# Layer 0 experts: context products gathered into fewer, longer groups on TensorE

## Chip, cores and metric

The kernel runs on one core of a Trainium2 chip. The metric is device microseconds (us) of one execution; lower is better. A profiled execution gives the rows that are quoted below. The engines are PE (TensorE, matrix products; its weight loads are listed as PEld), ACT (ScalarE), DVE (VectorE), POOL (GpSimd) and SP, whose queue issues most DMA loads.

## What is computed

A two-layer backbone over 1024 latent tokens and 256 context tokens of width 1024. Layer 0 mixes tokens with two recurrent head groups, layer 1 with attention, and each layer ends in a mixture of 16 experts. An expert picks its tokens itself (128 latent tokens and, in layer 0 alone, 32 context tokens), and adds its result to their rows:

```python
def expert_choice_ffn(h, w_router, w_gate, w_up, w_down):
    B, T, _ = h.shape
    cap = CAP_FACTOR * T // N_EXPERTS
    aff = jax.nn.softmax((h @ w_router).astype(jnp.float32), axis=-1)
    g, idx = lax.top_k(jnp.swapaxes(aff, 1, 2), cap)
    ...
    hid = jax.nn.silu(jnp.einsum('becd,edf->becf', xg, w_gate)) * jnp.einsum('becd,edf->becf', xg, w_up)
    y = jnp.einsum('becf,efd->becd', hid, w_down) * g[..., None].astype(h.dtype)
    return jnp.zeros_like(h).at[bidx, idx].add(y)
```

All arrays are float32. The three weights of an expert are 1024x1024 each, 12 MB together.

## The kernel before

**Chunks.** `experts` walks the 16 experts of a layer. An expert's weights come in twelve chunks of 1 MB, [128, 2048] in SBUF: for each half of the 1024 hidden columns a gate and an up chunk for the first 512 rows (q = 0) and for the last 512 (q = 1), eight in all, and then four down chunks. `weight_chunk` issues the load of a chunk on SP's queue into a raw buffer (`wc`), has ACT round it to fp32r (`wch`) and DVE subtract that from the raw chunk (`wcl`). The pair wch and wcl is called a split pair here. Raw buffers and split pairs are rings: a load waits until the last reader of the buffer's previous chunk is done, a split until the last product with the pair's previous chunk is done. Before, layer 0 has five raw buffers (`nraw`) and four split pairs (`nsplit`).

**Latent products.** The 128 latent tokens' products are made as three fp32r products per 128 weight rows (`mm3`, L138 to L140: high by high, high by low, low by high), each 128x128 by 128x512, into `acc`. A chunk takes 12 of them. They read the split pair alone. The text calls them A.

**Context products.** The 32 context tokens fill only 32 of the array's 128 columns. `mm_context` (L1143) multiplies them in fp32 straight with the raw chunk, and puts the products of even and odd k and of the two matrices m into four column strips (rows 0, 32, 64, 96 of `cg`), so that four run beside each other. Each fp32 product shows as two instructions in the trace. These read the raw buffers, and so hold them. The text calls a run of such products that stands between other work on PE a group, C.

**Order.** PE also transposes: the gathered tokens (`xg`, `xgc`), the hidden activations (`sil` of latent tokens, `hc` of context tokens), and it makes the next expert's row numbers from one-hot products (`rt_hot`, L1075). Every engine works through a fixed list in order; a scheduler makes the lists when the program is built, so that products may end up a little apart from where the code calls them. After the sixteenth expert PE makes part of layer 1's modulation (`mod`, L296, 32 columns wide too), and layer 1 begins with the rows that the last expert has added to (`ye`, then the scatter into `xl`). Layer 1's experts have no context products and run with three split pairs and thirteen raw buffers.

The ring of five raw buffers lies in a pool (`ring`) that exists before the experts' own pool; further raw buffers (`spare_chunk`, as many as `spare` says for the layer) lie in the experts' pool.

Of the kernel before, what the change touches and what calls it, by code (L numbers as in the profile page):

```python
# [23 lines left out]
KT = 8  # L24
# [85 lines left out]
class Kernel:  # L110
# [5 lines left out]
    every = 4  # L116
    xbufs, on_act, on_pool, zfirst, xfirst, nat = 10, (1, 5), (0, 2, 4, 6), 9, 0, 7
    pooled, gated = (2, 0), (0, 2)
    spare = (0, 5)
    ahead = 7  # L120
    by_act, by_pool = (1, 3, 5), (0, 2, 4)
    turned, eased = (0, 1), (2,)
# [1029 lines left out]
    def experts(self, l, routes, hs, xs, m5s, ring, pool, psum):  # L1152

        nc, io = self.nc, self.io
        two = len(routes) == 2
# [52 lines left out]
        def gate_up_chunk(e, half, q, w):  # L1208
            src = w[e, 512 * q:512 * q + 512, 512 * half:512 * half + 512].rearrange("(k p) f -> p k f", p=128)
            return self.weight_chunk(l, ring, pool, src, [128, 4, 512])  # L1210

        def wide_chunk(e, q, w):

            src = w[e, 256 * q:256 * q + 256, :].rearrange("(p a) f -> p a f", a=2)
            return self.weight_chunk(l, ring, pool, src, [128, 2, D])
# [12 lines left out]
        def gate_up(e, half, q, x, acc, cg):  # L1228
            xt, xct = x
            c = []  # L1230
            for m, w in enumerate((wg, wu)):
                c.append(early.pop(0) if early else gate_up_chunk(e, half, q, w))
                for kk in range(4):
                    k = 4 * q + kk
                    self.mm3(acc[:, m], (xt[0][:, k, :], xt[1][:, k, :]), (c[m][1][:, kk, :], c[m][2][:, kk, :]),
                             k == 0, k == KT - 1)
            if two:
                for kk in range(4):
                    k = 4 * q + kk
                    self.mm_context(cg, xct, [c[m][0][:, kk, :] for m in range(2)], k)  # L1240

        def both(acc):

# [31 lines left out]
        def down(e, q, ht, hct, acc, cy):  # L1275
            if two:
                src = wd[e, 256 * q:256 * q + 256, :].rearrange("(k p) f -> p k f", p=128)
                raw, hi, lo = self.weight_chunk(l, ring, pool, src, [128, 2, D])
            else:
                _, hi, lo = wide_chunk(e, q, wd)  # L1280
            for kk in range(2):
                k = 2 * q + kk
                for m in range(2):
                    o = slice(512 * m, 512 * m + 512)
                    self.mm3(acc[:, m], (ht[0][:, k, :], ht[1][:, k, :]), (hi[:, kk, o], lo[:, kk, o]),
                             k == 0, k == KT - 1)
            if two:
                for kk in range(2):
                    k = 2 * q + kk
                    self.mm_context(cy, hct, [raw[:, kk, 512 * m:512 * m + 512] for m in range(2)], k)  # L1290

        def add_rows(i, idx, gate, y, acc):
            nc.vector.scalar_tensor_tensor(y, acc, gate, m5s[i], op0=OP.mult, op1=OP.mult)  # L1293
            nc.gpsimd.indirect_dma_start(out=rows[i], out_offset=bass.IndirectOffsetOnAxis(ap=idx, axis=0),  # L1294
                                         in_=y, in_offset=None, compute_op=OP.add)

        picked = {}
        self.chunks = 0
        self.extra = [self.spare_chunk(l, pool) for _ in range(self.spare[l])]
        if not two:  # L1300
# [35 lines left out]
        for e in range(NE):  # L1336
            hct = pool.tile([128, KT, 32], F32, name="hct", bufs=2) if two else None
            accs = lambda: (psum.tile([128, 2, 512], F32, name="acc", tag="acc", bufs=2),
                            psum.tile([128, 512], F32, name="cg", tag="cg", bufs=2) if two else None)
            a0 = accs()  # L1340
            gate_up(e, 0, 0, x, *a0)
            if e + 1 < NE:
                nxt = pick(e + 1)
            gate_up(e, 0, 1, x, *a0)
            h0 = activate(*a0)
            a1 = accs()
            gate_up(e, 1, 0, x, *a1)
            ht = [pool.tile([128, KT, 128], F32R, name=f"ht{j}", bufs=1) for j in range(2)]
            turn(0, h0, ht, hct)
            gate_up(e, 1, 1, x, *a1)  # L1350
            h1 = activate(*a1)
            if e + 1 < NE:
                x = prep(*nxt)
            ay = accs()
            down(e, 0, ht, hct, *ay)
            turn(1, h1, ht, hct)
            for q in range(1, 4):
                down(e, q, ht, hct, *ay)
# [551 lines left out]
    def build(self, stop=None):  # L1910
        tc, io = self.tc, self.io
        pools = lambda stack, name, **kw: stack.enter_context(
            tc.tile_pool(name=name, bufs=1, reuse_waits="tile", **kw))
        pe = {mybir.EngineType.PE}
        with ExitStack() as ctx:
            self.ctx = ctx
            self.nraw, self.nsplit = 5, 4
            self.constants()
            self.xd = [self.scratch("xl", [TL, D]), self.scratch("xc", [TC, D])]
            self.hd = [self.scratch("hl", [TL, D]), self.scratch("hc", [TC, D])]  # L1920
            self.od = self.scratch("od", [8, 128, TL])
            self.qrd = self.scratch("qrd", [8, 8, 128, 64])
            raws = ExitStack()
            with ExitStack() as right:
                with ExitStack() as left:
                    pa = pools(left, "l0a")
                    ps = pools(left, "l0ps", space=PSUM)

                    class Twice:
                        def tile(self, shape, dt, name, tag, bufs=2):  # L1930
                            return ps.tile(shape, dt, name=name, tag=tag, bufs=2)
                    psum = Twice()
                    self.layer0(pa, psum)
                    if stop == "l0mix":
                        return
                    self.route_constants(pools(ctx, "rc", side="right"))
                    mc = pools(right, "m0c", side="right")
                    ring = pools(right, "m0r", side="right")
                    pool = pools(left, "m0m")
                    left.enter_context(tc.manual_schedule(engines=pe))  # L1940

                    def bank(kind):
                        tag = {"acc": "sA", "tp": "tp", "rl": "mm"}[kind]
                        return psum.tile([128, 2, 512] if tag == "sA" else [128, 512], F32, kind, tag)

                    rest = self.mod_round(1, 5, pool, psum, "mm", lambda: self.ring_chunk(ring), width=1024,
                                          tag="rx", bufs=2)
                    routes = self.tail(0, self.fetch_recurrent, self.wo, pool, bank, mc, pools(left, "m0t", side="right"), rest)
                if stop == "l0":
                    return  # L1950
                self.raws, self.wd_raw = pools(raws, "l1w"), []
                self.moe(0, routes, ring)
            self.layer1(raws)
            if stop == "mla":
                return
            with ExitStack() as right:
                mc = pools(right, "m1c", side="right")
                self.nraw, self.nsplit = self.nraw1, 3
                ring = pools(right, "m1r", side="right")
                with ExitStack() as left:  # L1960
                    pool = pools(left, "m1m")
                    psum = pools(left, "m1p", space=PSUM)
                    left.enter_context(tc.manual_schedule(engines=pe))
                    wo = [pool.tile([128, KT, D], F32R, name=f"wo{j}") for j in range(2)]
                    bank = lambda kind: psum.tile([128, 2, 512] if kind == "acc" else [128, 512], F32, name=kind,
                                                  bufs=2)
                    tags = ("rx", "rxm", "rx", "rxm", "rh", "m2", "m4", "m3")
                    stage = lambda k: pool.tile([128, D], F32, name="owr", tag=tags[k], bufs=1 if k > 3 else 2)
                    routes = self.tail(1, self.fetch_attention, wo, pool, bank, mc, pools(left, "m1t", side="right"),
                                       weights=self.out_weights(*wo, stage, io["w_o"][0]))  # L1970
                self.moe(1, routes, ring)
# [123 lines left out]
```

## Time and profile before

| what | us |
|---|---|
| median of 3 runs (lowest to highest) | 3352.9 (3351.01 to 3357.59) |
| the profiled execution's own time | 3350.71 |
| its span from first to last instruction | 3348.9 |
| first product of layer 0's experts to the last C | 1091.7 to 1923.9 |

The profiled execution is 2.2 us below the median, and its span lacks 1.8 us of its time. In the rows a time after an engine's name is a start in us from the span's beginning, then the duration; matmuls overlap, so what one costs is read from start to next start.

### The profile page before, as it was taken

To read this page: it belongs to the slowest core of one execution; us is meant where nothing else is said; L and a number is where in the kernel's file an instruction comes from. 1 tells how busy PE (TensorE), PEld (TensorE's weight loads), DVE (VectorE), ACT (ScalarE), POOL (GpSimd) and SP (SyncE) were. 2 spreads that over 40 slices of the span, in tenths; PEclk is the share of its full clock that TensorE was granted. 3 is DMA by queue.
4 is the path that set the end of the run, shared out by engine and by line. 5 is a ranking of instruction groups with operands and counts; after the bars stand their busy time and mean duration, and the time that the engine had idled before them with its cause. 6 is when DMAs were issued, how large, how long until landed. Compare 5 with 4: busy or idle time off the path is not lost.

```text
span 3348.9 us, 50379 instructions
## 1 busy us (share of the span) xinstructions
PE 3084.0 (92%) x19910; PEld 2370.4 (71%) x19910; DVE 2263.6 (68%) x3526; ACT 1681.5 (50%) x2405; POOL 653.8 (20%) x730
## 2 busy tenths in 40 slices
PE   5999989898896999999999979999998969999997
PEld 4878767786674566666666668888887758887775
DVE  4774463535657676776776666766666588988887
ACT  4444433544322465565555543555554247766675
POOL 3134452426212111111111010000000110111111
PEclk8999999999898999999999989999999979999999
DMA  6112144134753677878788732010005569999995
GB/s 209 47 32 61 42 151 151 43 100 170 259 175 127 223 263 266 267 275 266 270 272 265 270 97 53 23 29 22 19 15 187 192 244 373 374 363 355 372 358 185
DMA packets 252798, 624.92 MB, mean 187 GB/s; under 512 B 47876, under 2 KB 107482, under 8 KB 222866
## 3 DMA queue, kind: packets, MB, share of 16 engines
q1 hardware_dynamic: 227154, 545.17, 45.4%
q0 software_dynamic: 25408, 76.54, 8.1%
q8 instruction: 156, 2.56, 0.3%
q14 instruction: 80, 0.66, 0.1%
HBM read 560.71 MB, written 60.92 MB: 186 GB/s over the span
## 4 chain that ended last, share of the span: by engine, by line
PE 56%; DVE 4%; ACT 3%; DMA 2%; issue 2%; POOL 0%; SPq 0%; POOLq 0%; ACTq 0%; DVEq 0%
PE acc L138 12%; PE acc L140 11%; PE acc L139 11%; PE cg L1143 6%; PE tp L138 2%; PE tp L139 2%; PE tp L140 2%; PE tp L1784 2%; PE tp L1195 1%; PE tp L1265 1%; PE s L1753 1%; DVE wcl L145 1%; PE s L138 1%; PE s L140 1%; PE s L139 1%
## 5 line engine op out<-in xcount | busy, mean ns | idle before, releaser
L145 DVE TENSOR_TENSOR wcl<-wc,wch 128x2048 fp32r<-128x2048 f32 x380 | 874.1, 2308 | 258.6 <-ACT wch L144 257.3
L144 ACT ACTIVATE wch<-wc 128x2048 fp32r<-128x2048 f32 x380 | 727.9, 1919 | 430.1 <-PE acc L140 160.7
L139 PE MATMUL acc<-wcl,xt 128*128 128x512 f32 x1024 | 408.1, 399 | 1.9 <-DVE wcl L145 1.9
L138 PE MATMUL acc<-wch,xt 128*128 128x512 f32 x1024 | 405.1, 404 | 1.1 <-ACT xt L144 1.1
L140 PE MATMUL acc<-wch,xt 128*128 128x512 f32 x1024 | 405.8, 397 | 0.0
L138 PEld LDWEIGHTS acc<-wch,xt 128*128 128x128 f32 x1024 | 194.0, 189 | 72.3 <-issue 17.6
L139 PEld LDWEIGHTS acc<-wcl,xt 128*128 128x128 f32 x1024 | 193.7, 189 | 46.4 <-DVE wcl L145 4.0
L140 PEld LDWEIGHTS acc<-wch,xt 128*128 128x128 f32 x1024 | 193.4, 189 | 45.2
L139 PE MATMUL acc<-wcl,ht 128*128 128x512 f32 x512 | 204.8, 400 | 8.1 <-DVE wcl L145 8.1
L138 PE MATMUL acc<-wch,ht 128*128 128x512 f32 x512 | 211.5, 413 | 0.4 <-ACT wch L144 0.4
L140 PE MATMUL acc<-wch,ht 128*128 128x512 f32 x512 | 205.7, 402 | 0.0
L138 PE MATMUL mm<-ahi,w 128*128 128x512 f32 (+1 forms) x480 | 182.9, 381 | 0.0
L140 PE MATMUL mm<-ahi,w 128*128 128x512 f32 (+1 forms) x480 | 173.5, 362 | 0.0
L139 PE MATMUL mm<-alo,w 128*128 128x512 f32 (+1 forms) x480 | 173.5, 361 | 0.0
L1161 POOL DMA_INDIRECT xg<-hl,rt_i x32 | 83.1, 2596 | 422.9 <-issue 173.0
L1294 POOL DMA_INDIRECT xl<-ye,rt_i x31 | 69.7, 2249 | 468.5 <-DVE ye L1293 468.5
L138 PE MATMUL mm<-w,ahi 128*128 128x256 f32 (+1 forms) x480 | 148.5, 309 | 2.6 <-DVE tm L432 2.6
L144 ACT ACTIVATE pt<-tp 128x512 fp32r<-128x512 f32 (+1 forms) x192 | 98.5, 529 | 101.7 <-PE tp L1784 100.5
L145 DVE TENSOR_TENSOR pt<-tp,pt 128x512 fp32r<-128x512 f32 (+1 forms) x192 | 113.7, 594 | 44.8 <-ACT pt L144 44.7
L1143 PE MATMUL cg<-wc,xct 128*32 128x512 f32 x1024 | 138.7, 599 | 0.0
L140 PE MATMUL mm<-w,alo 128*128 128x256 f32 (+1 forms) x480 | 137.9, 287 | 0.0
L139 PE MATMUL mm<-w,ahi 128*128 128x256 f32 (+1 forms) x480 | 137.7, 287 | 0.0
(530 smaller groups left out, 7084.7 us busy)
## 6 DMA issues: line engine op xcount, KB each, us to landing
wc<-in_w_gate SPq DMA_DIRECT2D x128, 1024.0 KB, 7.5
wc<-in_w_up SPq DMA_DIRECT2D x128, 1024.0 KB, 6.0
wc<-in_w_down SPq DMA_DIRECT2D x128, 1024.0 KB, 5.7
w<-in_w_mod SPq DMA_DIRECT2D x32, 1024.0 KB, 5.0
craw<-in_w_in SPq DMA_DIRECT2D x40, 256.0 KB, 3.1
wm<-in_w_mod SPq DMA_DIRECT2D x8, 1024.0 KB, 10.6
wc<-in_w_mod SPq DMA_DIRECT2D x8, 1024.0 KB, 10.2
xl<-rxm POOLq DMA_DIRECT2D x16, 512.0 KB, 5.3
```

Source lines behind the costliest of these rows:

```text
L138: mm(out, a[0], b[0], start=first, stop=False, skip_group_check=skip)
L139: mm(out, a[0], b[1], start=False, stop=False, skip_group_check=skip)
L140: mm(out, a[1], b[0], start=False, stop=last, skip_group_check=skip)
L144: self.nc.scalar.activation(hi, src, AF.Copy)
L145: self.nc.vector.tensor_sub(lo, src, hi)
L1143: self.nc.tensor.matmul(out[g:g + 32, :], a[:, k, :], ws[m], start=(k < 2), stop=(k >= KT - 2), skip_group_check=True)
L1161: return nc.gpsimd.indirect_dma_start(out=out, out_offset=None, in_=src, in_offset=bass.IndirectOffsetOnAxis(ap=idx, axis=0))
L1195: nc.tensor.transpose(p[:, 128 * j:128 * j + 128], rows_of(xg[:, 512 * half:512 * half + 512], j), self.ident)
L1265: nc.tensor.transpose(p[:, 128 * j:128 * j + 128], rows_of(sil, j), self.ident)
L1294: nc.gpsimd.indirect_dma_start(out=rows[i], out_offset=bass.IndirectOffsetOnAxis(ap=idx, axis=0), in_=y, in_offset=None, compute_op=OP.add)
L1753: nc.tensor.matmul(out, qrl[:, q], krs[:, ks], start=False, stop=True)
L1784: nc.tensor.transpose(p[:, 128 * j:128 * j + 128], pr[:, 128 * (t0 + j):128 * (t0 + j) + 128], self.ident)
```

## The change

The context products no longer follow each pair of chunks. In `gate_up` the raw chunks of q = 0 are kept in a list (`held`), and after q = 1 all eight k are multiplied, 16 products in one call sequence where there were 8 and 8. In `down` the products of two chunks stand together, 8 where there were 4 and 4. To hold the raw chunks so long, three raw buffers are added (`spare` 0 to 3, eight in all), and one split pair is given up (`nsplit` 4 to 3). Nothing that is computed changes, and layer 1 is not touched.

```diff
-    spare = (0, 5)
+    spare = (3, 5)
...
-            if two:
-                for kk in range(4):
-                    k = 4 * q + kk
-                    self.mm_context(cg, xct, [c[m][0][:, kk, :] for m in range(2)], k)
+            held.extend(c)
+            if q:
+                for kk in range(KT):
+                    self.mm_context(cg, xct, [held[2 * (kk // 4) + m][0][:, kk % 4, :] for m in range(2)], kk)
+                held.clear()
...
             if two:
-                for kk in range(2):
-                    k = 2 * q + kk
-                    self.mm_context(cy, hct, [raw[:, kk, 512 * m:512 * m + 512] for m in range(2)], k)
+                held.append(raw)
+            if two and q % 2:
+                for kk in range(4):
+                    self.mm_context(cy, hct, [held[kk // 2][:, kk % 2, 512 * m:512 * m + 512] for m in range(2)],
+                                    2 * q - 2 + kk)
+                held.clear()
...
-        picked = {}
+        picked, held = {}, []
...
-            self.nraw, self.nsplit = 5, 4
+            self.nraw, self.nsplit = 5, 3
```

What it does to PE's list is seen best in an expert's down chunks. Before, a group of 4 products follows each chunk, and one lone product of the next expert's first chunk (`cg<-wc,xct`) has slipped in among the A of the third:

```order
L140 MATMUL acc<-wch,ht_11929 128x512
L1143 MATMUL cg<-wc,hct 32x512 x4
L138 MATMUL acc<-wch,ht_11928 128x512
L139 MATMUL acc<-wcl,ht_11928 128x512
L1143 MATMUL cg<-wc,xct 32x512
L140 MATMUL acc<-wch,ht_11929 128x512
L138 MATMUL acc<-wch,ht_11928 128x512
```

In the changed kernel the same place reads:

```order
L140 MATMUL acc<-wch,ht_11921 128x512
L1143 MATMUL cg<-wc,hct 32x512 x8
L138 MATMUL acc<-wch,ht_11920 128x512
L139 MATMUL acc<-wcl,ht_11920 128x512
L140 MATMUL acc<-wch,ht_11921 128x512
L138 MATMUL acc<-wch,ht_11920 128x512
```

Two groups have become one, and the lone product is gone. Written out for a middle expert, with the number of products behind each letter (T for transposes of sil, hc, xg and xgc, R for the one-hot products), PE's list before is A24 C7 R A24 C8 A24 C8 Tsil Thc A24 C8 Txg A11 Txgc A1 C4 Tsil A6 Thc A6 C4 A2 C1 A10 C4 A12 C4, and now A24 R A24 C16 A24 Tsil Thc A24 C16 Txg A7 Txgc A5 Tsil Thc A12 C8 A24 C8. Over all experts the 768 products stand in 143 groups before (64 of 4, 15 of 1, 15 of 7, 49 of 8) and in 64 now (32 of 16, 32 of 8).

The second place is SP's queue at the start of the experts. Lines with - are of before, with + of the change; `m` and `m5c` are modulation rows, `wdr` a small weight of layer 1:

```order
 L839 DMA m_10923<-mods 128x1024
-L1460 DMA m5c<-mods 64x1x512
-L1522 DMA wdr<-in_w_kr 128x64
-L1124 DMA wc<-in_w_up 128x4x512
-L1124 DMA wc<-in_w_gate 128x4x512
-L1124 DMA wc<-in_w_up 128x4x512
+L1464 DMA m5c<-mods 64x1x512
+L1124 DMA wc<-in_w_up 128x4x512
+L1124 DMA wc<-in_w_gate 128x4x512
+L1124 DMA wc<-in_w_up 128x4x512
+L1526 DMA wdr<-in_w_kr 128x64
```

The sixth to eighth chunk of the first expert are loaded into the new buffers ahead of `wdr`, without a wait on PE; before, the loads behind `wdr` waited for the first groups C.

## Rows read from the trace of the kernel before

**Rows 1.** Page: span; busy time, share of the span and instructions of TensorE.

```profile
span 3348.9 us, 50379 instructions
PE 3084.0 (92%) x19910; PEld 2370.4 (71%) x19910; DVE 2263.6 (68%) x3526; ACT 1681.5 (50%) x2405; POOL 653.8 (20%) x730
```

**Rows 2.** Page: the chain that ended last, share of the span by line.

```profile
PE acc L138 12%; PE acc L140 11%; PE acc L139 11%; PE cg L1143 6%; PE tp L138 2%; PE tp L139 2%; PE tp L140 2%; PE tp L1784 2%; PE tp L1195 1%; PE tp L1265 1%; PE s L1753 1%; DVE wcl L145 1%; PE s L138 1%; PE s L140 1%; PE s L139 1%
```

**Rows 3.** Busy time by stretch: layer 0's experts, then layer 1's (two stretches), then `mod`.

```profile
core 0: us, PE busy (x) PEld busy (x) DVE busy (x) ACT busy (x) POOL busy (x), PEclk, DMA share, GB/s
1462.00:1925.00 463.00, 462.81 (x2514) 287.24 (x2518) 326.77 (x272) 258.44 (x212) 63.84 (x33) 1.00 0.80 269
2770.00:2900.00 130.00, 130.00 (x610) 105.88 (x609) 118.23 (x87) 93.80 (x68) 15.40 (x8) 1.00 0.97 376
2900.00:3100.00 200.00, 196.78 (x905) 158.40 (x904) 175.36 (x121) 138.01 (x95) 29.24 (x11) 1.00 0.96 361
1924.00:1927.60 3.60, 3.58 (x68) 1.89 (x60) 1.88 (x3) 3.41 (x6) 2.57 (x2) 1.00 0.47 85
```

**Rows 4.** Timeline of PE in a middle expert's down chunks: start, duration, line.

```profile
1451.75 1.06 PE L1143 MATMUL cg<-wc,hct 128*32 128x512 f32 x8
1452.75 0.50 PE L138 MATMUL acc<-wch,ht 128*128 128x512 f32 x1
1453.09 0.40 PE L139 MATMUL acc<-wcl,ht 128*128 128x512 f32 x1
1453.41 1.05 PE L1143 MATMUL cg<-wc,xct 128*32 128x512 f32 x2
1454.39 0.50 PE L140 MATMUL acc<-wch,ht 128*128 128x512 f32 x1
1454.73 0.39 PE L138 MATMUL acc<-wch,ht 128*128 128x512 f32 x1
1454.96 0.39 PE L139 MATMUL acc<-wcl,ht 128*128 128x512 f32 x1
```

**Rows 5.** Timeline of PE in the same expert: a group with transposes behind it.

```profile
1431.47 0.40 PE L140 MATMUL acc<-wch,xt 128*128 128x512 f32 x1
1431.79 1.92 PE L1143 MATMUL cg<-wc,xct 128*32 128x512 f32 x16
1433.65 0.66 PE L1265 MATMUL tp<-ident,sil 128*128 128x128 f32 x4
1434.23 0.43 PE L1271 MATMUL tp<-ident,hc 32*128 32x32 f32 x4
1434.60 0.50 PE L138 MATMUL acc<-wch,xt 128*128 128x512 f32 x1
1434.93 0.39 PE L139 MATMUL acc<-wcl,xt 128*128 128x512 f32 x1
```

**Rows 6.** Timeline of PE in layer 1: one-hot products among A.

```profile
2922.11 0.40 PE L140 MATMUL acc<-wch,ht 128*128 128x512 f32 x1
2922.35 0.66 PE L1075 MATMUL tp<-pay,rt_hot 128*128 128x5 bf16 x8
```

**Rows 7.** Timelines of ACT and DVE in layer 1: one chunk's split; in brackets idle before.

```profile
2901.93 1.93 ACT L144 ACTIVATE wch<-wc 128x2048 fp32r<-128x2048 f32 x1 [0.90 <-PE acc L140]
2903.88 2.29 DVE L145 TENSOR_TENSOR wcl<-wc,wch 128x2048 fp32r<-128x2048 f32 x1 [0.30 <-ACT wch L144]
```

**Rows 8.** Timeline of PE in layer 1: the last A on that pair's previous chunk.

```profile
2901.49 0.40 PE L140 MATMUL acc<-wch,xt 128*128 128x512 f32 x1
```

**Rows 9.** Tile `wc`: issue of a load to its landing.

```profile
DMA to landing us min/median/max: 4.7/6.5/13.5
```

**Rows 10.** Timelines of PE and DVE at the start of layer 0's experts.

```profile
1096.53 1.03 PE L1203 MATMUL tp<-ident,xgc 32*128 32x32 f32 x8 [0.98 <-DMA xgc<-hc,idx]
1097.49 0.80 PE L140 MATMUL acc<-wch,xt 128*128 128x512 f32 x1
1081.76 9.21 DVE L145 TENSOR_TENSOR wcl<-wc,wch 128x2048 fp32r<-128x2048 f32 x1
```

## Prediction

> **What bounds the kernel now.** I read the page first: TensorE is busy for 92% of the span, more than any other engine [rows 1]. Next the chain that ended last, which says whether the end waits for that work: its largest shares are A, and behind them the context products of L1143 with 6%, some 200 us [rows 2]. [...]
>
> **What a group costs.** Durations of matmuls overlap, so I read from start to next start. One A follows another after 0.23 us (1454.73 to 1454.96). A group starts 0.32 us after the A ahead of it (1453.09 to 1453.41), 0.09 late. A group of 4 products holds PE for 1.00 us (1451.75 to 1452.75). Behind it the second A comes 0.34 us after the first (1452.75 to 1453.09), 0.11 late [rows 4]. A group of 8 holds PE for 1.86 us (1431.79 to 1433.65) [rows 5]. As four strips work beside each other, I call four products, one in each strip, a layer: the second layer costs 1.86 - 1.00 = 0.86 us. A group then has a fixed part, whatever its length: 0.09 + (1.00 - 0.86) + 0.11 = 0.34 us. The lone product holds PE for 0.98 us (1453.41 to 1454.39) [rows 4], so it costs a whole layer with three strips empty, and a fixed part besides.
>
> **The change, part by part.**
>
> *Groups.* The order has 143 groups before: 64 of one layer, 64 of two (49 of 8 and 15 of 7 products), 15 lone ones, hence 64 + 128 + 15 = 207 layers. Now it has 32 of four layers and 32 of two, 192 layers. Before: 207 x 0.86 + 143 x 0.34 = 226.6 us. Now: 192 x 0.86 + 64 x 0.34 = 186.9. That is 39.7 us less, 26.9 of it fixed parts and 12.9 the empty strips. Bounds: before has no group of more than two layers. If each third and fourth layer cost what a first one does (1.00), 64 of them would take back 9 us; I see no reason for less than 0.86. I take 0.86, which is one layer behind another, the nearest case.
>
> *Transposes and one-hot products.* Before, 47 runs of them (the sil transposes of both halves and the one-hot products) stand right behind a group and share its border. Now they stand between A. The entry is free: in layer 1 one-hot products start 0.24 us after an A, as another A would [rows 6]. The exit costs what a group's does, 0.33 instead of 0.23 (1434.60 to 1434.93) [rows 5]. So a group taken from in front of such a run saves its fixed part less that exit, and I give back 47 x 0.11 = 5.2 us. The ends are 3.4 us (sixteen runs of hc transposes, which had borders of their own, now stand with sil) and 16 us (47 x 0.34, if each paid a group's whole fixed part). I take 5.2, which is the border the rows show.
>
> *The end of the stage.* Layer 1 waits for the last expert's sum, which needs its last A; the last group stands behind that. It now holds two layers instead of one, so 0.9 us more lies off the path.
>
> *Three split pairs instead of four.* ACT's rounding of a chunk now waits for the last A on the chunk three places earlier. Layer 1 shows this case: the last A starts at 2901.49, ACT at 2901.93, DVE at 2903.88, and DVE is through 2.29 us later, at 2906.17 [rows 7, 8]. From that last A to a full pair are 4.68 us; PE works meanwhile on the two other pairs, 24 x 0.23 = 5.5 us. This leaves 0.8 us at each chunk, in runs of four chunks without a group; behind every such run there is now a group of four layers, 1.00 + 3 x 0.86 = 3.6 us, in which PE uses no pair and both splitters catch up. Behind the waiting ACT instruction stand ACT's own copies and roundings for `sc`, `sil`, `ht`, `xt`, for which PE's transposes and the down chunks wait. How much PE loses is bounded by layer 1, which runs A almost without pauses on three pairs: nothing in the 130 us from 2770 (130.00 busy) with DVE at 91%, and 3.2 of 200 us from 2900 [rows 3]. Over 16 experts of some 50 us ((1923.9 - 1091.7) / 16 = 52 now) these are 0 and 13 us. I take 3, nearer to nothing, since the groups are pauses that layer 1 lacks and DVE stays near 74% (326.77 us of work in 463 less some 20).
>
> *Eight raw buffers.* Raw chunks are now freed four at once, at the end of a long group, and four loads start together. The tightest is the first down chunk, whose buffer comes free at the end of the expert's first long group. Until its first A, PE has 24 A, the transposes of sil and hc (0.95 us and their exit [rows 5]), 24 A and another long group: 5.5 + 1.1 + 5.5 + 3.6 = 15.7 us. A split takes 4.68 less the 0.44 of the release, so the chunk may land 11.4 us after the group. Loads land after 6.5 us in the median, 13.5 at most [rows 9], and the others follow at 376 GB/s [rows 3], 2.8 us for each MB, while PE needs 2.8 us and more for each chunk. So the loads are hidden by two stretches of A and a group; were that cover gone, each expert would wait for the late part of one load. The bounds are 0 and (13.5 - 11.4) x 16 = 34 us; I take nothing, as the median lies 5 us inside.
>
> *The start.* Before, PE's second A stood until 1097.49 behind the xgc transposes, which waited for a gather [rows 10]. Now those come after 13 A, and the second half of xt's split on DVE no longer stands behind a chunk's split of 2.3 us. Against that, three loads of 1 MB now run at the time of the first gathers, 3 x 2.8 = 8.4 us of DMA; DVE's long subtraction (9.21 us from 1081.76) hides most of it [rows 10]. From this come -2 to +4 us; I take +1.
>
> **Sum.** 39.7 - 5.2 + 0.9 - 3 - 0 + 1 = 33.4 us. The profiled execution took 3350.7 us (its span and 1.8 us around it), so 3317.3; the median of the runs is 2.2 us above it, so I forecast 3319.5, say 3319.
>
> **Rivals.**
>
> *A little starving (three pairs hold PE up now and then).* For it: in the run of four chunks that opens an expert, DVE also has the last expert's `ye`, `sc` and `yce`, and its 0.5 us to spare per chunk (2.8 - 2.29) are 2 us there. Against it: the two splits ahead of that run fall into the last down group. With 0.6 us lost in each of the 32 runs of four chunks, 19 us stand in place of the 3, and the time is 3335.
>
> *Slower: ACT's queue stands.* When a rounding waits for PE, everything behind it on ACT waits too, and if PE then waits for one of these (ht ahead of the down chunks), they wait for each other in turn. A loss of one chunk's A, 12 x 0.23 = 2.8 us, in each expert is 45 us in place of the 3, so 3361. It turns the sign from 33.4 / 16 = 2.1 us an expert. For it: ACT waits 0.90 us for A at a chunk in layer 1 [rows 7]. Against it: the same queue there costs PE at most 1.6%.
>
> *Late loads.* If the four loads that start together run toward the slowest landing, the first down chunk of each expert comes up to 2.1 us late; half of the 34 us gives 3336.
>
> *More than forecast.* If PE never starves, transposes give back only 3.4 and the start gains 4, the sum is 39.7 - 3.4 + 0.9 + 4 = 41.2, so 3312.
>
> [...]
>
> That the change doesn't gather the products is no rival: the order shows 64 groups.
>
> **How the numbers follow.** As forecast 0.70, a little starving 0.14, late loads 0.05, more 0.05, ACT's queue 0.05, the clock 0.01. The forecast's own range is 3312 to 3328: one way no starving, the small give-back and the good start (7 us), the other the layers' 9 us. To hold the time 8 times in 10 I leave out the two slow cases and the worse half of starving and late loads: 3310 to 3338. No change within 0.2% (6.7 us, about what a measurement of this kernel can tell) would be 3346 to 3360; starving or late loads twice as bad reach it, 0.04 and 0.01 of their chances, together 0.05. Slower by more takes ACT's queue or the clock: 0.06. Faster: 0.89.
>
> **What would show it.** In the changed profile: PE still busy all the time from some 1105 on; groups of 16 products that hold PE for 3.6 us and of 8 for 1.9; an expert every 50 us, some 2 us less than now; A behind long groups at 0.23. The forecast is wrong if PE shows waits for `wch` or `wcl` of more than 10 us in this stage, if ACT waits for loads of down chunks just before PE runs dry, or if a third layer takes clearly more than 0.86 us.

## The result, and the profile after

The changed kernel takes 3312.32 us (median of 4 runs, 3311.28 to 3314.29), before 3352.56 beside it: a ratio of 0.9881, 95% interval 0.9869 to 0.9892, 40.2 us less. A second series (below, 3308.36 against 3352.12) gives 0.9869, 0.9851 to 0.9887, 43.8 us less. The forecast was 3319 in a range of 3310 to 3338, so the first series lies inside, near the case of 3312 in which PE never starves, and the second 1.6 us below the range's lower end. The page of the changed kernel, for [rows 1], and the chain by line of its execution in the second series, for [rows 2]:

```profile
span 3309.5 us, 50386 instructions
PE 3051.5 (92%) x19910; PEld 2382.1 (72%) x19910; DVE 2264.7 (68%) x3526; ACT 1683.3 (51%) x2405; POOL 683.7 (21%) x730
```

```profile
PE acc L138 12%; PE acc L139 12%; PE acc L140 12%; PE cg L1143 5%; PE tp L138 2%; PE tp L139 2%; PE tp L140 2%; PE tp L1788 2%; PE tp L1195 1%; DVE wcl L145 1%; PE s L1757 1%; PE s L138 1%; PE s L140 1%; PE s L139 1%; PE s L1756 1%
```

The same 19910 instructions keep PE busy 32.5 us less, and in this chain C has gone from 6% to 5%. The chain of the first series' execution can't be compared: followed back from layer 1's start it leads along POOL, which gathers the experts' rows and adds their results, through the whole stage (PE 35%, issue 20%, no C among its largest shares). That the bound is still PE, as [rows 3] show it for before, is read from the stage itself. The stretch of [rows 3], now ending with the stage at 1880, shows no idle time at all and the clock at 1.00:

```profile
1462.00:1880.00 418.00, 418.00 (x2364) 276.65 (x2363) 311.15 (x255) 247.08 (x201) 78.11 (x29) 1.00 0.81 280
```

PE's timeline in a middle expert, for [rows 4]: a group of 16 products with the transposes of xg behind it, and the first down group, now of 8.

```profile
1369.79 0.40 PE L140 MATMUL acc<-wch,xt 128*128 128x512 f32 x1
1370.12 3.64 PE L1143 MATMUL cg<-wc,xct 128*32 128x512 f32 x32
1373.69 1.09 PE L1195 MATMUL tp<-ident,xg 128*128 128x128 f32 x8
...
1382.11 1.92 PE L1143 MATMUL cg<-wc,hct 128*32 128x512 f32 x16
1383.96 0.50 PE L138 MATMUL acc<-wch,ht 128*128 128x512 f32 x1
1384.30 0.39 PE L139 MATMUL acc<-wcl,ht 128*128 128x512 f32 x1
```

Four layers hold PE for 3.57 us (1370.12 to 1373.69), two for 1.85: a third and a fourth layer cost 0.86 each, as a second does. The borders are the old ones, 0.33 in (1369.79 to 1370.12) and 0.34 out. The same transposes as in [rows 5], now between A:

```profile
1363.19 0.40 PE L140 MATMUL acc<-wch,xt 128*128 128x512 f32 x1
1363.43 0.60 PE L1266 MATMUL tp<-ident,sil 128*128 128x128 f32 x4
1363.95 0.43 PE L1272 MATMUL tp<-ident,hc 32*128 32x32 f32 x4
1364.32 0.50 PE L138 MATMUL acc<-wch,xt 128*128 128x512 f32 x1
1364.66 0.40 PE L139 MATMUL acc<-wcl,xt 128*128 128x512 f32 x1
```

Going in is free (0.24), coming out costs 0.11, as the prediction had it. What ACT waits for has changed, though. Waits of ACT in the experts' stage (us in total, times, longest), changed kernel first, then before:

```profile
ACT wch L144 <- PE acc L140: 168.9, 123, 2.9
```

```profile
ACT wch L144 <- DMA wc<-in_w_up: 151.5, 59, 8.8
ACT wch L144 <- DMA wc<-in_w_gate: 47.5, 40, 3.3
ACT wch L144 <- DMA wc<-in_w_down: 41.7, 33, 2.4
ACT wch L144 <- PE acc L140: 13.9, 2, 7.0
```

Before, the roundings came as late as the loads let them (240.7 us of waits); with eight raw buffers they wait for the split pair instead, and for no load that the profile names (for another 40.9 us of their idle time it names nothing). None of it reaches PE now: PE has no wait behind the start. Before, two of the late loads did:

```profile
PE acc L139 <- DVE wcl L145: 1.6, 2, 1.4
```

**Where the 40 us are.** Executions differ by some us ahead of the experts and behind them, so I measure the stage alone, from the transpose of `tf` (L1100), the last of PE's work that both kernels do in the same place, to the last A. These two and the 24th A, before:

```profile
1082.14 0.20 PE L1100 MATMUL tp<-ident,tf 16*32 16x16 f32 x1 [5.83 <-ACT tf L1097]
1103.80 0.40 PE L140 MATMUL acc<-wch,xt 128*128 128x512 f32 x1
...
1922.73 0.40 PE L140 MATMUL acc<-wch,ht 128*128 128x512 f32 x1
```

and now, with the rest of the start:

```profile
1082.05 0.20 PE L1100 MATMUL tp<-ident,tf 16*32 16x16 f32 x1 [5.84 <-ACT tf L1097]
1087.57 1.09 PE L1195 MATMUL tp<-ident,xg 128*128 128x128 f32 x4 [5.31 <-DMA xg<-hl,rt_i]
1093.09 0.78 PE L140 MATMUL acc<-wch,xt 128*128 128x512 f32 x1
1097.63 0.68 PE L1203 MATMUL tp<-ident,xgc 32*128 32x32 f32 x8
1100.68 0.40 PE L140 MATMUL acc<-wch,xt 128*128 128x512 f32 x1
1107.20 3.64 PE L1143 MATMUL cg<-wc,xct 128*32 128x512 f32 x32
...
1881.17 0.40 PE L140 MATMUL acc<-wch,ht 128*128 128x512 f32 x1
```

The stage took 840.6 us and takes 799.1, 41.5 less (the spans differ by 39.4; what lies behind the last A took 1424 to 1428 us in the executions of this document, whatever the kernel). An expert takes 49.40 us, from the group at 1107.20 to that of the seventh expert at 1403.61, divided by six. At the start the gather for xg now lands 3 us later, beside three more loads (PE waits 4.4 to 5.4 us for it in the eleven traces with seven or eight raw buffers, 1.6 to 2.3 in the three with five). But the 24th A stands at 1100.68, where before it stood at 1103.80 with `tf` 0.09 later: 3.0 us gained. The transposes of xgc no longer stop PE [rows 10], and the second half of xg's start 2.4 us earlier behind `tf` (1091.97; before 1094.47, behind a wait for the token numbers `idx`).

### The profile page after: what moved, and what is told of

Read it like the earlier page. It is cut to its first block, busy times and chain, and to the rows that moved or that the text cites. A ratio compares the mean times of both kernels' runs of the same rounds, so it can differ in the third digit from the quotient of the medians.

```text
span 3309.5 us, 50386 instructions
## 1 busy us (share of the span) xinstructions
PE 3051.5 (92%) x19910; PEld 2382.1 (72%) x19910; DVE 2264.7 (68%) x3526; ACT 1683.3 (51%) x2405; POOL 683.7 (21%) x730
## 4 chain that ended last, share of the span: by engine, by line
PE 35%; issue 20%; DVE 5%; POOL 4%; ACT 3%; DMA 2%; SPq 0%; POOLq 0%; ACTq 0%; DVEq 0%
PE acc L139 7%; PE acc L140 7%; PE acc L138 7%; PE tp L138 2%; PE tp L139 2%; PE tp L140 2%; PE tp L1788 2%; POOL xl L1298 1%; POOL xc L1298 1%; DMA xl<-ye,rt_i 1%; POOL xg L1161 1%; PE s L1757 1%; PE s L138 1%; PE s L140 1%; PE s L139 1%
## 5 line engine op out<-in xcount | busy, mean ns | idle before, releaser
L1298 POOL DMA_INDIRECT xl<-ye,rt_i x31 | 103.1, 3326 | 457.8 <-DVE ye L1297 457.8
L1161 POOL DMA_INDIRECT xg<-hl,rt_i x32 | 75.4, 2356 | 400.6 <-issue 176.1
L138 PE MATMUL acc<-wo,ot 128*128 128x512 f32 x288 | 120.2, 417 | 5.1 <-ACT wo L144 5.1
```

Of the source, the lines that this page charges most:

```text
L138: mm(out, a[0], b[0], start=first, stop=False, skip_group_check=skip)
L1161: return nc.gpsimd.indirect_dma_start(out=out, out_offset=None, in_=src, in_offset=bass.IndirectOffsetOnAxis(ap=idx, axis=0))
```

## The experiments

My theory was the prediction's: PE's list is the bound, a group has a fixed part of 0.34 us, a layer costs 0.86 however many strips work, and the buffers only make the long groups possible. The rivals were that the buffers themselves give much of the gain (ACT's waits for loads are gone), and that the long groups do, as pauses for ACT and DVE. The stage column is read as above, from one execution each.

| run | groups | stage us | median us | to before beside it |
|---|---|---|---|---|
| before | 143 | 840.6 | 3352.56 | |
| changed | 64 | 799.1 | 3312.32 | -40.2 |
| changed, second series | 64 | 799.1 | 3308.36 | -43.8 |
| buffers only | 144 | 831.1 | 3344.09 | -7.1 |
| gate and up gathered | 96 | 809.9 | 3319.23 | -31.9 |
| down gathered | 97 | 808.2 | 3320.56 | -30.6 |
| down in groups of 16 | 48 | 799.1 | 3308.52 | -42.6 |
| the same, cut into 5 and 11 | 64 | 811.7 | 3318.99 | -33.1 |
| down in 16, ht covered | 48 | 792.7 | 3301.03 | -51.1 |
| half of the products | 64 | 717.7 | 3232.64 | -119.5 |
| seven raw buffers | 64 | 798.5 | 3309.60 | -41.5 |
| five raw buffers | 186 | 882.5 | 3394.71 (one run) | +43.6 |
| two split pairs | 176 | 894.2 | 3407.56 (one run) | +56.5 |
| five raw, groups whole | 64 | 975.3 | 3492.56 (two runs) | +136.3 |

**Buffers only.** The kernel before with the new buffers:

```diff
-    spare = (0, 5)
+    spare = (3, 5)
-            self.nraw, self.nsplit = 5, 4
+            self.nraw, self.nsplit = 5, 3
```

> The kernel before with eight raw buffers and three split pairs, its products in the old order: 64 groups of 8, 48 of 4, and 16 more of 4 that the transposes of xgc cut into 1 and 3, so 208 layers. Theory (the gain is PE's list, buffers only permit it): nothing but the two waits for late loads that the trace of before shows inside the experts (2 us together) and the earlier start (some 3 us) go, one more layer comes: 3348 to 3350 us. Rival (the buffers are a good part of the gain, as ACT's 240 us of waits for loads vanish with them): 3340 or less. Second rival (three pairs starve PE where groups are short): above 3353.

Measured: 3344.09 (eight runs, 3339.0 to 3351.3), ratio 0.9975, 0.9964 to 0.9985. That lies between the two. The stage is 9.5 us shorter than before: 3.0 at the start, 2.0 for the two waits, and 4.5 that I had not counted, since the order came out otherwise too. The lone product now stands against the transposes of xgc (one product, xgc, three products), and PE has 160 stretches of A with borders where before had 175. Fifteen borders of 0.20 us make 3.0 of the 4.5, and one more group with one more layer takes 1.0 back; the other 2.5 I have not traced. So the buffers give 5 us by themselves and 9.5 of the 41.5 with the order that the scheduler made for them: not most of the gain, but more than I expected. Three pairs cost nothing even with short groups: PE has no wait behind the start.

**One half of the gathering each.** The changed kernel with the down products back behind each chunk, and then with the gate and up products back behind each pair of chunks:

```diff
-            if two:
-                held.append(raw)
-            if two and q % 2:
-                for kk in range(4):
...
+            if two:
+                for kk in range(2):
+                    k = 2 * q + kk
+                    self.mm_context(cy, hct, [raw[:, kk, 512 * m:512 * m + 512] for m in range(2)], k)
```

```diff
-            held.extend(c)
-            if q:
-                for kk in range(KT):
...
+            if two:
+                for kk in range(4):
+                    k = 4 * q + kk
+                    self.mm_context(cg, xct, [c[m][0][:, kk, :] for m in range(2)], k)
```

> The changed kernel with the down products back in groups of 4 behind each chunk: 96 groups, 192 layers. Theory (each group between A's has a fixed part of 0.34 us, whatever its length): 32 groups more than the changed kernel's 64, 32 x 0.34 = 10.9 us, so 3323 us, 29 below before. Rival (what counts are the lone products and their empty strips, which are gone here too): within 3 us of the changed kernel, 3312 to 3315.

> The changed kernel with the gate and up products back in groups of 8 behind each pair of chunks: 97 groups, 193 layers, no lone product. Theory: 33 groups more and a layer more than the changed kernel, 33 x 0.34 + 0.9 = 12.1, less the border that 31 runs of transposes and one-hot products share with a group again (31 x 0.11 = 3.4), plus 15 runs of hc transposes that stand apart (1.7): 10.4, so 3322 to 3323 us. Rival (the long groups of 16 are where it comes from, by more than their fixed part, since ACT and DVE catch up in them): 3330 or more.

Measured: 3319.23 (ratio 0.9902, 0.9887 to 0.9917) and 3320.56 (0.9908, 0.9895 to 0.9922). The stages are 10.8 and 9.1 us longer than the changed kernel's, where 10.9 and 10.4 were expected; the medians came out 1 to 4 us below the expected ones. Neither rival holds: the groups of the down chunks, which never had an empty strip, are worth as much as the theory says, and without any group of 16 nothing more is lost than the fixed parts.

**All of down in one group.** The eight k of the four down chunks together, tied behind the expert's last A (`end`):

```diff
-            if two and q % 2:
-                for kk in range(4):
-                    self.mm_context(cy, hct, [held[kk // 2][:, kk % 2, 512 * m:512 * m + 512] for m in range(2)],
-                                    2 * q - 2 + kk)
+            if two and q == 3:
+                with self.tc.issue_after(end.ins):
+                    for kk in range(KT):
+                        self.mm_context(cy, hct, [held[kk // 2][:, kk % 2, 512 * m:512 * m + 512] for m in range(2)], kk)
```

> The changed kernel with all four down chunks' products in one group of 16 at the end of the expert: 48 groups, all of 16, 192 layers. Theory: 16 groups fewer, 16 x 0.34 = 5.4 us, and two layers more of the last group lie off the path, 1.7 us: 3305 us. Rival (four down chunks held to the expert's end come free too late, and the loads behind them hold PE up): 3320 or more, with PE waiting for wch or wcl.

Measured: 3308.52 (0.9867, 0.9852 to 0.9882), and a stage as long as the changed kernel's. The groups did save their part (47 ahead of the last A hold PE for 167.8 us, the changed kernel's 63 for 171.8, and 16 pairs of borders less, some 7 us), but something took as much back: 4.7 us of waits, and 2.0 us that the one-hot products just ahead of the waiting A hold PE longer. PE's waits, PE's timeline, and DVE's:

```profile
PE acc L140 <- DVE ht L145: 4.7, 16, 0.7
```

```profile
1379.82 0.60 PE L1266 MATMUL tp<-ident,sil 128*128 128x128 f32 x4
...
1384.08 0.67 PE L1075 MATMUL tp<-pay,rt_hot 128*128 128x5 bf16 x8
1384.96 0.50 PE L140 MATMUL acc<-wch,ht 128*128 128x512 f32 x1 [0.22 <-DVE ht L145]
```

```profile
1382.02 2.29 DVE L145 TENSOR_TENSOR wcl<-wc,wch 128x2048 fp32r<-128x2048 f32 x1 [0.90 <-ACT wch L144]
1384.22 0.68 DVE L145 TENSOR_TENSOR ht<-tp,ht 128x512 fp32r<-128x512 f32 x1
```

The wait is not for a chunk. The low half of `ht` stands on DVE behind a chunk's 2.29 us and is done 5 us after the transposes of sil begin, and the third down chunk needs it. The group of 8 that stood in between hid that; it was cover, not cost alone. In my theory I had priced the group and not what it hid.

**Covering ht.** The same, with the transposes of xgc moved behind those of sil and hc, so that 0.6 us of other work stands between (`prep` then leaves them out, and `prep_context` makes them):

```diff
             if e + 1 < NE:
-                x = prep(*nxt)
+                x = prep(*nxt, True)
             ay = accs()
             down(e, 0, ht, hct, *ay)
             turn(1, h1, ht, hct)
+            if e + 1 < NE:
+                x = (x[0], prep_context(x[1]))
```

> All down products in one group of 16, as in the run that came to 3308.5, and the transposes of xgc moved behind those of sil and hc. In that run PE waits 16 times some 0.3 us for DVE's half of ht, as the group of 8 that stood ahead of the third down chunk in the changed kernel is gone. Theory (this wait took the gain of the merged groups): with 0.6 us of transposes and an exit between the two, the waits for ht vanish, 5 to 6 us: 3303 us, 47 to 48 below before, 7 to 8 below the changed kernel. Rival (the late loads of the four held chunks took it): no change from the 3308.5.

> The changed kernel itself, run beside the next three so that few us can be compared: 3310 to 3313 us; 40 us below before.

Measured side by side: 3301.03 (0.9854, 0.9834 to 0.9874) and 3308.36 (0.9869, 0.9851 to 0.9887), 7.3 us apart, as expected; the stage is 6.4 us shorter. One wait for `ht` is left of sixteen, 0.7 us. The intervals of the two ratios overlap, and one of the four executions took 3309.2, so the times alone don't settle it; the stage and the waits that are gone say where it gains.

**A layer with empty strips.** All of down called at the end without the tie; the order then puts five products after the second of the third chunk's A and eleven at the end:

> All four down chunks' products called at the expert's end, with nothing that holds them together: the order puts 5 of them after the second of the third chunk's A and 11 at the end. As many groups as the changed kernel (64), but one layer more per expert, as the fifth product stands alone in its layer and its three neighbours in another: 208 layers. Theory (a layer costs 0.86 us whether one strip works or four): 16 x 0.86 = 13.8 us more than the changed kernel, less 0.9 of the last group that lies off the path: 3325 us. Rival (only the number of groups and of products counts): as the changed kernel, 3311 to 3313.

Measured: 3318.99 (0.9906, 0.9891 to 0.9921), 10.6 above the changed kernel beside it; the stage is 12.5 us longer. The group of five:

```profile
1385.03 0.40 PE L139 MATMUL acc<-wcl,ht 128*128 128x512 f32 x1
1385.35 1.90 PE L1143 MATMUL cg<-wc,hct 128*32 128x512 f32 x10
1387.19 0.50 PE L140 MATMUL acc<-wch,ht 128*128 128x512 f32 x1
```

Five products hold PE for 1.84 us, eight for 1.85: the fifth costs a whole layer with three strips empty. The groups are as many as in the changed kernel, and up to the last A they hold PE for 184.2 us instead of 171.8, so the difference is the layers' alone.

**Half of the products.** Four of an expert half's eight k, and half of each down chunk's, are left out, in the same 64 groups, each tied behind the last A of its chunks (`end`):

```diff
-                for kk in range(KT):
-                    self.mm_context(cg, xct, [held[2 * (kk // 4) + m][0][:, kk % 4, :] for m in range(2)], kk)
+                with self.tc.issue_after(end.ins):
+                    for n in range(4):
+                        self.mm_context(cg, xct, [held[2 * (n // 2) + m][0][:, n % 2, :] for m in range(2)], n)
...
```

> The changed kernel with half of the context products left out (four of eight k in each half of the columns, and half of each down chunk's), in the same 64 groups of half the length: 96 layers. The context rows are then not the reference's. Theory (a layer costs 0.86 us and PE alone is the bound): 96 x 0.86 = 82.6 us less than the changed kernel, 3229 us, groups of 8 holding PE for 1.86 us and of 4 for 1.00. Rival (the long groups are also the pauses in which ACT, DVE and loads catch up, so that shorter groups give their time back as waits for wch and wcl): 3250 or more.

Measured: 3232.64 (0.9644, 0.9626 to 0.9662), 75.7 below the changed kernel of the same series, with a stage 81.4 us shorter (its profiled execution reached `tf` 6 us later than the changed kernel's, ahead of the change). The 95 layers that are gone ahead of the last A make 95 x 0.86 = 81.7, and the groups hold PE for 81.5 us less. PE has no wait behind the start: at 44 us an expert the splits and loads still keep up, so the long groups were not needed as pauses.

**Fewer buffers.** The changed kernel with seven and with five raw buffers (`spare` 2 and 0), and with two split pairs (`nsplit` 2):

> The changed kernel with seven raw buffers instead of eight. The eighth chunk's load then waits for the expert's first long group, and PE wants this chunk after the transposes and three chunks' A, 0.9 + 3 x 2.8 = 9.3 us behind that group; a load at the median (6.5 us) and its split (4.24) take 10.7. Theory (the loads are hidden with eight by little more than a chunk's time): 1.4 us late in each expert, 23 us, so 3333 us; with the slowest landing (13.5) 130 us, so up to 3440. Rival (loads are hidden widely, as the order of the raw buffers has slack): as the changed kernel, 3308 to 3313.

> The changed kernel's products and pairs with the five raw buffers of before. Four are held until a long group, so one chunk is there behind it, and the next starts to load when the group ends. Theory (the buffers are what lets the groups be long): behind each long group PE waits 10.7 - 0.9 - 2.8 = 7.0 us for the second chunk, and some 2 us behind the down groups, 16 us in each expert, 260 us in all: about 3570 us, well above before, with ACT's waits for loads and PE's waits for wch and wcl. Rival (the groups pay for the waits): below before, 3353.

> The changed kernel with two split pairs instead of three. A pair is full 4.68 us after the last A that read it, and PE has only the other pair's 2.8 us of A meanwhile. Theory (a pair's round trip of 4.68 us against the A between decides, and with three pairs 5.5 us of A cover it): 1.9 us lost at each of the eight chunks of an expert that no group stands ahead of, less some 3 us that the transposes cover, 12 us an expert, 197 us: about 3505 us. Rival (ACT's and DVE's lists leave room, the pairs never bound the kernel): below 3330.

Seven: 3309.60 (0.9869, 0.9852 to 0.9886), as with eight. The rival is right, and rows show why. SP, PE and ACT of that run:

```profile
1357.61 0.37 SPq L1124 DMA_DIRECT2D wc<-in_w_up  x1
```

```profile
1355.64 3.64 PE L1143 MATMUL cg<-wc,xct 128*32 128x512 f32 x32
1359.21 0.50 PE L138 MATMUL acc<-wch,xt 128*128 128x512 f32 x1
```

```profile
1362.79 1.92 ACT L144 ACTIVATE wch<-wc 128x2048 fp32r<-128x2048 f32 x1 [1.06 <-DMA wc<-in_w_up]
```

The load starts at 1357.61, in the middle of the group that I had it wait for to its end: the group's first half reads the first two chunks, whose buffers then come free 1.6 us early. It lands in 5.2 us instead of 6.5.

Five raw buffers and two pairs cost 83 and 95 us of the stage, where I had expected 260 and 197; neither the theory's time nor the rival's came. The profile shows neither of the mechanisms: behind the start PE waits once with five buffers, 0.6 us, and not at all with two pairs. Instead the order is another one. PE with five buffers:

```profile
1446.91 1.90 PE L1143 MATMUL cg<-wc,xct 128*32 128x512 f32 x10
1448.74 0.50 PE L138 MATMUL acc<-wch,xt 128*128 128x512 f32 x1
1449.17 1.06 PE L1143 MATMUL cg<-wc,xct 128*32 128x512 f32 x6
1450.16 0.66 PE L1195 MATMUL tp<-ident,xg 128*128 128x128 f32 x4
1450.75 1.05 PE L1143 MATMUL cg<-wc,xct 128*32 128x512 f32 x2
```

There are 186 groups, and with the same products some 60 layers more, as many strips stay empty. The groups hold PE for 241.4 us instead of 171.8; these 69.6 and the borders are the 83. With two pairs it is the same: 176 groups that hold PE for 251.2 us. I take it that the scheduler that writes the lists puts products wherever its own reckoning sees a late chunk, and that the lone product before [rows 4] is of the same kind; its reckoning itself is not on record.

**Five raw buffers with whole groups** tells whether the late loads are there at all:

```diff
             held.extend(c)
             if q:
+                with self.tc.issue_after(end.ins):
...
             if two and q % 2:
+                with self.tc.issue_after(end.ins):
...
...
-    spare = (3, 5)
+    spare = (0, 5)
```

> Five raw buffers as in the run that came to 3394.7 us, where PE never waited but the order had broken the 64 groups into 186; here each group is tied behind the last A of its chunks, so that it stays whole: 32 groups of 16 and 32 of 8. Theory (the late loads are there, and the order only turned them into broken groups): behind the first long group the second chunk comes 3.4 us late (its load issued 1.8 us before the group's end, 5.2 to land, 4.24 to split, against 2.8 of A and 1.4 of transposes), the third 0.4, behind the second long group 2.5: 6.3 us an expert, 101 us, so about 3410 us, with PE or its weight loads waiting for wch and wcl. Rival (the order broke them needlessly, as seven buffers were as good as eight): 3330 or less.

Measured: 3492.56, ratio 1.0407, 1.0372 to 1.0441, well above the theory's 3410 too. The late loads are there. PE's waits for chunks up to 1980, its timeline, and the stage in three stretches:

```profile
PE acc L139 <- DVE wcl L145: 64.4, 32, 2.8
PE acc L138 <- ACT wch L144: 13.6, 18, 1.9
```

```profile
1449.91 0.50 PE L139 MATMUL acc<-wcl,ht 128*128 128x512 f32 x1 [2.80 <-DVE wcl L145]
...
1452.17 0.63 PE L140 MATMUL acc<-wch,ht 128*128 128x512 f32 x1
1452.60 0.63 PE L138 MATMUL acc<-wch,ht 128*128 128x512 f32 x1
```

```profile
1110.00:1462.00 352.00, 314.94 (x1620) 205.59 (x1616) 214.72 (x180) 170.59 (x140) 46.71 (x22) 0.90 0.67 229
1462.00:1880.00 418.00, 374.21 (x1938) 244.55 (x1931) 262.03 (x217) 206.43 (x168) 60.30 (x28) 0.91 0.68 229
1880.00:2050.00 170.00, 152.26 (x785) 100.18 (x784) 106.01 (x81) 84.73 (x68) 15.43 (x7) 0.93 0.67 235
```

PE is idle 98.6 of 940 us, close to the 101 expected, though 11 of them are waits for DVE's `hct`; but the stage is 176 us longer than the changed kernel's. The granted clock is 0.90 to 0.93 in the mean of these stretches, and behind many of the waits, not all, A follow each other after 0.43 us instead of 0.23. The other 78 us, from start to next start without the waits: A behind A takes 68 more, of which 242 pairs at 0.43 make 242 x 0.2 = 48, and the groups, the ways into them and the transposes take the rest. The tie has also moved transposes and one-hot products in the order, so that how much of this is the loads' alone stays open. In any case the broken groups of the run before, at 83 us, were cheaper than these waits.

## Why the prediction was right, and where it was not

| term | forecast | measured |
|---|---|---|
| layers and the groups' 0.14, the last group off the path | 12.9 + 11.1 + 0.9 = 24.9 | 24.3 |
| borders of groups, less the transposes' give-back | 15.8 - 5.2 = 10.6 | 12.2 |
| starving with three pairs | -3 | 0 |
| late loads | 0 | +2.0 |
| start | +1 | +3.0 |
| sum, at the last A | 33.4 | 41.5 |

The first measured row sums every group of the two traces up to the last A, from its start to the start of what follows (196.0 and 171.8 us); the second is what is left of 41.5.

**Groups.** Right in mechanism and size. The runs with half of the gathering, with the cut layer and with half of the products each test one part (fixed part, empty strip, layer), and agree with 0.34 and 0.86 to within 2 us. What causes the fixed part no run here shows. Going in, only work of another shape in the rows than A's starts late: in the changed kernel's stage context products (128*32) and transposes of xgc (32*128) start 0.31 to 0.34 us after an A, transposes of sil and one-hot products (128*128) after 0.23 to 0.24. The shape can't be all of the fixed part: the 0.11 of coming out is nearly as large behind work of A's own shape on the array (0.32 us from the first A to the second behind one-hot products and transposes of xg, 0.34 behind a group) and as large behind a mere wait, as the longest one before shows:

```profile
1325.71 0.50 PE L139 MATMUL acc<-wcl,xt 128*128 128x512 f32 x1 [1.45 <-DVE wcl L145]
1326.05 0.39 PE L140 MATMUL acc<-wch,xt 128*128 128x512 f32 x1
```

**Transposes.** The step that was mis-sized is the give-back of 5.2. The prediction had the lower end, 3.4, for the case that sixteen runs of hc transposes join those of sil; the order showed that they do, for all but one expert, and I chose the upper count nevertheless. With 3.4 the row is 12.4.

**Three pairs.** The 3 us were nothing. ACT does wait for the last A on the pair three places earlier, 168.9 us in 123 waits, and PE, behind the start, for nothing. The order may have told it beforehand: the runs with five raw buffers and with two pairs suggest that this scheduler breaks groups where it reckons with a late chunk, and in the changed kernel's list all 64 are whole.

**Raw buffers.** Rightly put at nothing, on too tight a reckoning: buffers come free inside a group, and one of the eight is to spare. What the sum left out is that before had late loads of its own that reached PE, 2.0 us (1.6 of idle time and the slower start of A behind the two waits).

**The start** gave 3.0 us, inside the -2 to +4, where I had taken +1.

**The rivals.** ACT's queue did stand (168.9 us), which the second rival made its case, but nothing that PE wanted stood behind it. The clock, which the prediction gave 0.01, stayed at 1.00 through groups of 3.6 us; in the last experiment, where PE was idle 98.6 of 940 us, it was 0.90 to 0.93 in the means of the three stretches. What came is nearest to the fourth rival, 3312, and for its reasons: no starving, the small give-back, a good start. It had a chance of 0.05.

The two us between 41.5 in the stage and 39.4 in the span of the first series went behind the last A, in layer 1, which the change doesn't touch; the second series had them back (1425.5 us behind the last A, as before's 1426.3).

## What to carry to other kernels

Where small products stand among large ones, price a visit as a fixed part and a length, both from start to next start, and gather visits as far as the buffers let the operands wait; here 0.34 us and 79 visits were more than half of 40 us. Ask of each group that goes away what it hid: the middle down group covered a chain of 5 us on DVE, and without it the next gathering gave nothing until something else stood there. Where a scheduler fills gaps, a scarce buffer may show not as a wait but as broken groups, so read the order beside the waits.

## What the hardware showed

- In the changed kernel's stage, sil transposes and one-hot products (128*128 in the rows) start 0.23 to 0.24 us after an A, like another A (0.22 to 0.25); xgc transposes (32*128) and context products (128*32) start after 0.31 to 0.34. Behind a group, or a run of transposes or one-hot products, the second A follows the first after 0.31 to 0.35 us, and behind the two waits of before after 0.34 and 0.35.
- A layer of four fp32 products, each 128x32 by 512 columns in a strip of its own, cost 0.86 us as the second, third or fourth of a group (8 products held PE for 1.85 us, 16 for 3.57), and as much with three strips empty (5 products, 1.84).
- With five raw buffers and whole groups PE was idle 98.6 of 940 us, for up to 2.8 at a time, at a mean granted clock of 0.90 to 0.93, and behind the start 242 of 2146 pairs of A stood 0.43 us apart, 48 us more than at 0.23; in the changed kernel, at 1.00, none of 2131 did.
